# Scores of 64 contraction rows in row halves of TensorE, weights times values alternating between heads, and decay levels without their masked blocks

## The chip, the cores and the metric

The kernel runs on one core of one Trainium2 chip. The metric is the device time of one launch in microseconds, taken as the median of several runs. TensorE does the matrix products, VectorE (DVE in the profile), ScalarE (ACT) and GpSimd (POOL) the elementwise work, and SyncE (SP) issues the DMAs.

## The reference

The input is one sequence of 256 tokens of width 1024. Two transformer layers come first, each with modulation vectors from `silu(c) @ w_mod`, layer norms and a SwiGLU feed-forward; then one hybrid layer with 16 meta tokens in front, and a final norm. All of it is float32. Four places matter here.

- Layer 0, stick-breaking attention (8 heads of 64): `z = q k^T / 8` for the past keys, and the weights are `exp(log_sigmoid(z) + suffix sum of log_sigmoid(-z))`, then weights times values.
- Layer 0, DSA attention (8 heads of 64 with one shared key and value): an index score, `sum over 4 index heads of relu(q_idx k_idx^T) * w`, selects 64 keys for each query, and a softmax over those follows.
- Layer 1, differential attention (8 heads, two components of 64 each): `softmax(q0 k0^T) - lam * softmax(q1 k1^T)`, causal, times values of width 128.
- The hybrid layer's gated recurrence (8 heads of 128): `S_t = diag(f_t) S_{t-1} + k_t v_t^T`, `o_t = S_t^T q_t`.

```
s = einsum('bqhcd,bshcd->bhcqs', q, k) * d ** -0.5
p = softmax(where(causal, s, -inf))
a = p[:, :, 0] - lam * p[:, :, 1]
```

## The kernel before

Activations are kept transposed: channels on the 128 partitions, tokens in the free dimension. A weight slab (128 x 2048) is loaded by DMA into `stage`, split into a high part `whi` (ScalarE) and a rest `wlo` (VectorE), and each projection does three products per block of 128 channels (`mm3`, `group`, `gemm_pair`); the first seven slabs are loaded whole and multiplied in plain f32. The attention products are plain f32 too, which TensorE runs as two records each.

The order of the work isn't the order of the source. Every operation goes to `Plan.record`, which notes its engine, an estimate of its cost, its dependences and its place; `Plan.order` then simulates the engines, and on each takes the ready operation with the lowest place (with a small part for the length of what hangs on it); `issue` emits them in that order at line 433, so nearly all rows of the profile bear that line. Attention is written as generators (`gen_topk`, `gen_dsa`, `gen_sb`, `gen_diff`, `gen_hgrn`); `spin(3)` between the projections takes three steps of the oldest generator, and `BIAS` shifts the places of its operations (75 for the top-k, DSA and decay generators, 0 for stick-breaking and differential scores). The planner counts writes to one PSUM bank as dependent on each other; all eight banks are one pool, `pa`. SBUF tiles come from pools too: `w4` (19 of 1096 columns), `w2` (5 of 512), `w1`, `sm`.

The places that the change touches:

- Scores of two heads (or components) of 64 rows are one product over all 128 rows. The moving operand is a zero-padded block tile: `kz_d`, `kz_i` (lines 954 to 966), `qz` (1082 to 1093) and `kz` (1284 to 1298) hold one head's 64 rows in one half of the columns and the other's in the other half, with zeros between (GpSimd memsets). `gen_topk` (992), `gen_dsa` (1055), `gen_sb` (1128, 1129) and `gen_diff` (1249) use them. A mask is added to the scores in PSUM by a bf16 product with the identity.
- Products of weights and values for two heads write the two halves of the output partitions of one bank (1071 to 1075, 1150 to 1155), head by head.
- `gen_diff` handles one head in four steps (two query tiles, each with scores and softmax, then transposes).
- `gen_hgrn` builds the decayed attention matrix in levels of block size B = 1 to 64 within tiles of 128 tokens (1524 to 1552): for each level `Xt` holds decayed keys in the even blocks and decayed queries in the odd ones, eight products `Xt^T Xt` (128 x 128) go into two banks, and two masked copies (`copy_predicated` with `msk`) take the blocks that belong to the level.

Of the kernel before, what the change touches and what calls it, by code (L numbers as in the profile page):

```python
# [14 lines left out]
ALU = mybir.AluOpType  # L15
# [44 lines left out]
BUFS = {'w4': 19, 'w2': 5, 'w1': 11, 'sm': 16, 'stage': 3, 'mst': 3, 'whi': 6, 'wlo': 6}  # L60
# [45 lines left out]
class Plan:  # L106
# [74 lines left out]
    def cost(self, eng, op, writes, reads):  # L181
# [255 lines left out]
def kernel(ctx, tc, io, out):  # L437
# [516 lines left out]
    kz_t = w4("kzt")  # L954
    kz_d = kz_t[:, 0:512]
    kz_i = kz_t[:, 512:1024]
    G.memset(kz_t[:, 0:1024], 0.0)
# [6 lines left out]
    for a, kz, r0 in ((0, kz_d, 0), (1, kz_i, 64)):  # L964
        for b in range(2):
            V.tensor_add(kz[b * 64:b * 64 + 64, b * S:(b + 1) * S], t1[r0:r0 + 64, 0, :], t2[r0:r0 + 64, 0, :])
# [18 lines left out]
    def gen_topk():  # L985
        for t in range(2):
            nk = 128 * (t + 1)
            s = bias[:, t, :]
            for c in range(2):
                ps = bank("ps_i")  # L990
                o = two(ps[:, :2 * nk])
                T.matmul(o, qi[:, c * S + t * 128:c * S + t * 128 + 128], two(kz_i)[:, :, :nk], start=True, stop=True)
                r = two(w2("rl")[:, :2 * nk])
                A.activation(r, o, AF.Relu)
                for a in range(2):
                    if c == 0 and a == 0:
                        V.tensor_scalar(s[:, :nk], r[:, 0, :], wix[:, t, 0:1], 0.0, op0=ALU.mult, op1=ALU.add)
                    else:
                        V.scalar_tensor_tensor(s[:, :nk], r[:, a, :], wix[:, t, 2 * c + a:2 * c + a + 1], s[:, :nk],
# [48 lines left out]
    def gen_dsa():  # L1048
        for t in range(2):
            nk = 128 * (t + 1)  # L1050
            PT = [w4c(f"pt{t}{i}", S) for i in range(t + 1)]
            for j in range(4):
                ps = bank("ps_i")
                o = two(ps[:, :2 * nk])
                T.matmul(o, qd[j // 2][:, (j % 2) * S + t * 128:(j % 2) * S + t * 128 + 128], two(kz_d)[:, :, :nk],
                         start=True, stop=False)
                T.matmul(o, identb, biasb[:, t, None, :nk].to_broadcast([128, 2, nk]), start=False, stop=True)
                e = two(w2("e"))
                ls = softmax_pair(e, o, nk)
                for a in range(2):  # L1060
                    if a < EACT:
                        A.activation(e[:, a, :nk], e[:, a, :nk], AF.Copy, scale=ls[:, a:a + 1])
                    else:
                        V.tensor_scalar(e[:, a, :nk], e[:, a, :nk], ls[:, a:a + 1], None, op0=ALU.mult)
                for st in range(t + 1):
                    pt = bank("ps_t")
                    for a in range(2):
                        T.transpose(pt[:, a * 128:a * 128 + 128], e[:, a, st * 128:st * 128 + 128], ident)
                    A.activation(PT[st].rearrange("p j (a q) -> p a j q", a=2)[:, :, j, :], two(pt[:, :256]), AF.Copy)
                yield  # L1070
            ps = bank("ps_o")
            for a in range(2):
                for st in range(t + 1):
# [50 lines left out]
    def gen_sb():  # L1124
        for j in range(4):
            qzj = two(qz[j // 2][:, (j % 2) * 512:(j % 2) * 512 + 512])
            za, zb = bank("ps_z"), bank("ps_z")
            T.matmul(two(za), ks[:, j, 0:128], qzj, start=True, stop=False, skip_group_check=True)
            T.matmul(two(zb[:, :256]), ks[:, j, 128:256], qzj[:, :, 128:256], start=True, stop=False, skip_group_check=True)
            for ap in (two(za)[:, :, 0:128], two(zb[:, :256])):  # L1130
                T.matmul(ap, identb, strib[:, None, :].to_broadcast([128, 2, 128]), start=False, stop=True,
                         skip_group_check=True)
            sp = w4("sp")
            A.activation(sp[:, 0:512], za, AF.Abs)
            A.activation(sp[:, 512:768], zb[:, :256], AF.Abs)
            A.activation(sp[:, :768], sp[:, :768], AF.Exp, scale=-1.0)
            A.activation(sp[:, :768], sp[:, :768], AF.Ln, bias=1.0)
            V.scalar_tensor_tensor(sp[:, 0:512], za, 0.0, sp[:, 0:512], op0=ALU.max, op1=ALU.add)
            V.scalar_tensor_tensor(sp[:, 512:768], zb[:, :256], 0.0, sp[:, 512:768], op0=ALU.max, op1=ALU.add)
            yield  # L1140

            T.matmul(za, C("tn"), sp[:, 0:512], start=False, stop=False, skip_group_check=True)
# [728 lines left out]
```

## Time and profile before

| | |
|---|---|
| median of 3 runs | 1158.2 us (1157.85 to 1158.86) |
| profiled execution, its own time | 1161.2 us |
| its span, first to last instruction | 1159.4 us |
| mean granted TensorE clock | 0.99 |
| TensorE busy | 1127.6 us, 97% |
| weight loads busy | 1079.3 us, 93% |
| VectorE busy | 912.1 us, 79% |
| ScalarE busy | 723.1 us, 62% |

PE is the matrix product itself, PEld the loading of its stationary operand. A matmul's record lasts beyond its place in the pipeline, so the pace is read from start to start and not from the record's length. A chain of waits is followed back from the last instruction to what released each step. Tiles are named by their pool: `pa` is any PSUM bank, `w` any working tile, `cst` the constants.

### The profile page before, as it was taken

How to read it: one execution, taken by the hardware profiler on the slowest of the kernel's cores; microseconds unless marked ns; L12 is line 12 of the kernel's file. 1: busy time of each engine (PE TensorE's matmuls, PEld its weight loads, DVE VectorE, ACT ScalarE, POOL GpSimd, SP SyncE). 2: the span in 40 equal slices, each digit the busy share in tenths (PEclk: the TensorE clock that was granted, in tenths of full speed). 3: DMA queues.
4: the chain of work that ended last, by engine and by line, in shares of the span. 5: the costliest groups of instructions: out<-in, count | busy, mean ns of one | idle time of the engine just before them, and what ended most of it. 6: DMA issues, size and time to landing. Idle time of an engine off the chain costs nothing.

```text
span 1159.4 us, 21967 instructions
## 1 busy us (share of the span) xinstructions
PE 1127.6 (97%) x8787; PEld 1079.3 (93%) x8787; DVE 912.1 (79%) x1764; ACT 723.1 (62%) x1314; POOL 12.4 (1%) x18
## 2 busy tenths in 40 slices
PE   5999999999999899999999999999999999999997
PEld 4886799999998779999999999999999999999996
DVE  6799899888989899995557696996579886767652
ACT  3558677444459987764445377876757765555541
POOL 1010000000010000000000000000000000000000
PEclk9999999999999999999999999999999998999998
DMA  9938748998983244585554524344433434555441
GB/s 349 411 125 316 258 146 326 331 338 308 338 327 121 87 168 146 200 309 183 178 200 168 198 82 173 120 165 156 180 110 124 168 110 146 207 187 184 169 164 37
DMA packets 42247, 232.27 MB, mean 200 GB/s; under 512 B 4641, under 2 KB 6177, under 8 KB 24097
## 3 DMA queue, kind: packets, MB, share of 16 engines
q1 hardware_dynamic: 42144, 230.87, 54.9%
q8 instruction: 69, 1.13, 0.4%
q14 instruction: 34, 0.27, 0.1%
HBM read 229.81 MB, written 1.05 MB: 199 GB/s over the span
## 4 chain that ended last, share of the span: by engine, by line
PE 82%; DVE 9%; ACT 5%; DMA 3%; issue 1%; SPq 0%; DVEq 0%; ACTq 0%
PE pa L433 82%; DVE w L433 5%; ACT w L433 4%; DMA mst<-in_wmod_dram 2%; DVE wlo L433 2%; DVE mst L433 1%; ACT whi L433 1%; DVE sm L433 1%; DMA w<-in_pos_dram 1%; DMA w<-in_xT_dram 1%; DVE stage L433 0%; SPq L433 0%; ACT sm L433 0%; DVE mw L433 0%; DVEq L1867 0%
## 5 line engine op out<-in xcount | busy, mean ns | idle before, releaser
L433 PE MATMUL pa<-w,whi 128*128 128x256 f32 (+4 forms) x5104 | 920.3, 288 | 9.3 <-DMA whi<-in_w_dram 7.4
L433 PEld LDWEIGHTS pa<-w,whi 128*128 128x128 f32 x5104 | 771.2, 190 | 18.5 <-ACT w L433 6.7
L433 PE MATMUL pa<-w,wlo 128*128 128x256 f32 (+3 forms) x2608 | 665.7, 290 | 2.2 <-DVE wlo L433 2.2
L433 ACT ACTIVATE whi<-stage 128x1024 fp32r<-128x1024 f32 (+1 forms) x330 | 338.7, 1041 | 254.8 <-PE pa L433 226.6
L433 PEld LDWEIGHTS pa<-w,wlo 128*128 128x128 f32 x2608 | 467.2, 190 | 9.0 <-DVE wlo L433 4.0
L433 DVE TENSOR_TENSOR wlo<-stage,whi 128x1024 fp32r<-128x1024 f32 (+1 forms) x330 | 392.8, 1201 | 93.1 <-ACT whi L433 90.8
L433 ACT ACTIVATE w<-w 128x256 fp32r<-128x256 f32 (+9 forms) x257 | 117.1, 468 | 71.6 <-DVE w L433 68.0
L433 DVE TENSOR_TENSOR w<-w,w 128x256 fp32r<-128x256 f32 (+6 forms) x323 | 144.8, 465 | 10.9 <-ACT w L433 9.0
L433 ACT ACTIVATE w<-pa 128x256 f32<-128x256 f32 (+12 forms) x298 | 108.0, 390 | 47.1 <-PE pa L433 41.4
L433 DVE SCALAR_TENSOR_TENSOR mst<-mst,scb 128x1024 f32<-128x1024 f32 x90 | 108.7, 1221 | 9.2 <-DMA mst<-in_wmod_dram 8.9
L433 DVE TENSOR_TENSOR w<-w,pa 128x256 f32<-128x256 f32 (+2 forms) x146 | 58.7, 418 | 56.7 <-PE pa L433 52.0
L432 ACT ACT_TABLE_LOAD x61 | 78.3, 1283 | 1.8 <-PEq L1861 0.7
L433 PE MATMUL pa<-w,w 128*128 128x128 f32 (+8 forms) x340 | 68.6, 334 | 3.0 <-issue 1.6
L433 PEld LDWEIGHTS pa<-w,w 128*128 128x128 f32 (+4 forms) x340 | 41.9, 174 | 13.1 <-issue 7.1
L433 PE MATMUL pa<-cst,w 128*128 128x1 f32 (+4 forms) x236 | 38.8, 255 | 3.3 <-ACT w L433 3.3
L433 PEld LDWEIGHTS pa<-cst,w 128*128 128x128 f32 (+2 forms) x236 | 29.0, 158 | 10.0 <-ACT w L433 6.1
L433 PE MATMUL pa<-w 128*128 128x128 f32 x240 | 34.6, 275 | 0.0
L433 PE MATMUL pa<-whi,w 128*128 128x512 f32 x96 | 32.6, 423 | 0.0
L433 PEld LDWEIGHTS pa<-w 128*128 128x128 f32 x240 | 31.3, 191 | 0.0
L433 DVE SCALAR_TENSOR_TENSOR w<-pa,vec,w 128x256 f32<-128x256 f32 (+1 forms) x48 | 23.1, 483 | 6.6 <-PE pa L433 5.7
L433 DVE SCALAR_TENSOR_TENSOR w<-pa,mod,w 128x256 f32<-128x256 f32 x32 | 15.0, 481 | 14.8 <-PE pa L433 14.8
L433 DVE COPY_PREDICATED w<-msk,pa 128x512 f32<-128x512 uint8 x28 | 20.5, 737 | 3.9 <-PE pa L433 3.8
(144 smaller groups left out, 478.1 us busy)
## 6 DMA issues: line engine op xcount, KB each, us to landing
mst<-in_wmod_dram SPq DMA_DIRECT2D x90, 512.0 KB, 5.5
stage<-in_wgu_dram SPq DMA_DIRECT2D x44, 1024.0 KB, 5.0
stage<-in_wi_dram SPq DMA_DIRECT2D x36, 1024.0 KB, 4.8
stage<-in_wup_dram SPq DMA_DIRECT2D x22, 1024.0 KB, 4.8
stage<-in_wd_dram SPq DMA_DIRECT2D x24, 896.0 KB, 4.5
stage<-in_w_dram SPq DMA_DIRECT2D x15, 1024.0 KB, 6.7
stage<-in_wo_dram SPq DMA_DIRECT2D x12, 1024.0 KB, 4.8
stage<-in_wd_dram SPq DMA_DIRECT2D x12, 1024.0 KB, 5.4
```

Of the source, the lines that this page charges most:

```text
L432: self.nc.scalar.preload_act_table_set(tables[i])
L433: fn(*[real(a) for a in args], **{k: real(a) for k, a in kw.items()})
```

## The change

Scores: `scores` makes two products of 64 rows per pair of heads, one on partitions 0 to 63 and one on 64 to 127, into two banks (one per head); two pairs share the two banks. The zero-padded tiles and their memsets go. `gen_diff` takes two heads in one generator of six steps; DSA takes two pairs together. Products of weights and values are written alternately for the two heads. A decay level multiplies the first 128 - B columns of `Xt` with its odd blocks alone, eight products of 64 columns into one bank, with one masked copy. The planner halves its estimate for f32 products of 64 rows, and pool `w2` has six buffers.

```diff
-BUFS = {'w4': 19, 'w2': 5, ...
+BUFS = {'w4': 19, 'w2': 6, ...
...
-                return max(214.0, 4 * n / 2.4 + 5)
+                return max(214.0, 4 * n / 2.4 + 5) / (2 if reads[0].shape[0] == 64 else 1)
...
+    def scores(o, c, left, right, stop=False):
+        for a in range(2):
+            r = slice(a * 64, a * 64 + 64)
+            T.matmul(o[a][:, c, :], left[r], right[r], start=c == 0, stop=stop, skip_group_check=True)
...
-    kz_t = w4("kzt")
-    kz_d = kz_t[:, 0:512]
-    kz_i = kz_t[:, 512:1024]
-    G.memset(kz_t[:, 0:1024], 0.0)
+    kz_d, kz_i = w2("kd2")[:, :S], w2("ki2")[:, :S]
...
+            o = [two(bank("ps_i")[:, :2 * nk]) for _ in range(2)]
             for c in range(2):
-                ps = bank("ps_i")
-                o = two(ps[:, :2 * nk])
-                T.matmul(o, qi[:, c * S + t * 128:c * S + t * 128 + 128], two(kz_i)[:, :, :nk], start=True, stop=True)
+                scores(o, c, qi[:, c * S + t * 128:c * S + t * 128 + 128], kz_i[:, :nk], c == 1)
...
-            for j in range(4):
-                ps = bank("ps_i")
-                o = two(ps[:, :2 * nk])
-                T.matmul(o, qd[j // 2][:, (j % 2) * S + t * 128:(j % 2) * S + t * 128 + 128], two(kz_d)[:, :, :nk],
-                         start=True, stop=False)
-                T.matmul(o, identb, biasb[:, t, None, :nk].to_broadcast([128, 2, nk]), start=False, stop=True)
-                e = two(w2("e"))
-                ls = softmax_pair(e, o, nk)
...
+            for i in range(2):
+                o = [two(bank("ps_i")[:, :2 * nk]) for _ in range(2)]
+                for c in range(2):
+                    scores(o, c, qd[i][:, c * S + t * 128:c * S + t * 128 + 128], kz_d[:, :nk])
+                es = []
                 for a in range(2):
...
+                    T.matmul(o[a], identb, biasb[:, t, None, :nk].to_broadcast([128, 2, nk]), start=False, stop=True,
+                             skip_group_check=True)
+                    e = two(w2("e"))
+                    ls = softmax_pair(e, o[a], nk)
...
-            for a in range(2):
-                for st in range(t + 1):
+            for st in range(t + 1):
+                for a in range(2):
                     T.matmul(ps[a * 64:a * 64 + 64, :].rearrange("p (j q) -> p j q", j=4), vtok[:, st, 0:64],
...
-    qz = [w4("qz0"), w4("qz1")]
-    ks = w4c("ksb", S)
-    for i in range(2):
-        G.memset(qz[i], 0.0)
+    qs, ks = w4c("qsb", S), w4c("ksb", S)
...
-            ps = two(next_pair())
-            for c in range(2):
-                for a in range(2):
-                    A.activation(qz[i][a * 64:a * 64 + 64, c * 512 + a * S:c * 512 + a * S + S], ps[a * 64:a * 64 + 64, c, :],
-                                 AF.Copy, scale=0.125)
+            ps = next_pair()
+            A.activation(qs[:, 2 * i:2 * i + 2, :], two(ps), AF.Copy, scale=0.125)
...
-            T.matmul(two(za), ks[:, j, 0:128], qzj, start=True, stop=False, skip_group_check=True)
-            T.matmul(two(zb[:, :256]), ks[:, j, 128:256], qzj[:, :, 128:256], start=True, stop=False, skip_group_check=True)
...
+            z = [bank("ps_z") for _ in range(2)]
+            for a in range(2):
+                r = slice(a * 64, a * 64 + 64)
+                T.matmul(z[a][:, 0:256], ks[r, j, 0:128], qs[r, j, :], start=True, stop=False, skip_group_check=True)
+            for a in range(2):
+                r = slice(a * 64, a * 64 + 64)
+                T.matmul(z[a][:, 256:384], ks[r, j, 128:256], qs[r, j, 128:256], start=False, stop=False, skip_group_check=True)
...
             for a in range(2):
                 h = 2 * j + a
-                T.matmul(ps[a * 64:a * 64 + 64, 0:256], vsb[:, 0, h * 64:h * 64 + 64], w[:, a * 256:a * 256 + 256],
+                T.matmul(ps[a * 64:a * 64 + 64, 0:256], vsb[:, 0, h * 64:h * 64 + 64], w[:, a * 384:a * 384 + 256],
                          start=True, stop=False, skip_group_check=True)
+            for a in range(2):
+                h = 2 * j + a
                 T.matmul(ps[a * 64:a * 64 + 64, 128:256], vsb[:, 1, h * 64:h * 64 + 64],
-                         w[:, 512 + a * 128:512 + a * 128 + 128], start=False, stop=True, skip_group_check=True)
+                         w[:, a * 384 + 256:a * 384 + 384], start=False, stop=True, skip_group_check=True)
...
-    def gen_diff(h, q, kz):
+    def gen_diff(h, qk):
...
+            o = [two(bank("ps_i")[:, :2 * nk]) for _ in range(2)]
+            for c in range(2):
+                scores(o, c, qk[c][:, 0, t * 128:t * 128 + 128], qk[c][:, 1, :nk])
+            es = []
+            for a in range(2):
+                T.matmul(o[a][:, :, t * 128:nk], identb, causb[:, None, :].to_broadcast([128, 2, 128]), start=False,
+                         stop=True, skip_group_check=True)
+                e = two(w2("e"))
+                es.append((e, softmax_pair(e, o[a], nk)))
+            (e0, l0), (e1, l1) = es
+            for c in range(2):
+                V.tensor_scalar(e1[:, c, :nk], e1[:, c, :nk], l1[:, c:c + 1], nlam, op0=ALU.mult, op1=ALU.mult)
+                V.scalar_tensor_tensor(e0[:, c, :nk], e0[:, c, :nk], l0[:, c:c + 1], e1[:, c, :nk], op0=ALU.mult, op1=ALU.add)
             yield
...
-            G.memset(kzt[:, 0:1024], 0.0)
...
-        V.tensor_add(q, parts[0][0], parts[0][1])
-        for a in range(2):
-            V.tensor_add(kz[a * 64:a * 64 + 64, a * S:a * S + S], parts[1][0][a * 64:a * 64 + 64],
-                         parts[1][1][a * 64:a * 64 + 64])
-        bg.append((gen_diff(h, q, kz), BIAS["diff"]))
+        if h % 2 == 0:
+            qk0 = qk
+        else:
+            bg.append((gen_diff(h - 1, (qk0, qk)), BIAS["diff"]))
...
-                for hp in range(2):
-                    ps = bank("ps_h")
-                    for a in range(2):
-                        for t in range(2):
-                            xs = Xt[:, 2 * hp + a, t * 128:t * 128 + 128]
-                            T.matmul(ps[:, (a * 2 + t) * 128:(a * 2 + t) * 128 + 128], xs, xs, start=True, stop=True,
-                                     skip_group_check=True)
-                    V.copy_predicated(quads(At, hp), msk[:, None, lv * 128:lv * 128 + 128].to_broadcast([128, 4, 128]),
-                                      ps.rearrange("p (a b) -> p a b", b=128))
-                    yield
+                n = 128 - B
+                ps = bank("ps_h")[0:n, :].rearrange("p (q i b) -> p q i b", q=8, b=B)
+                for h in range(4):
+                    for t in range(2):
+                        xs = Xt[:, h, t * 128:t * 128 + 128]
+                        T.matmul(ps[:, 2 * h + t], xs[:, 0:n], xs.rearrange("p (i c b) -> p c i b", c=2, b=B)[:, 1],
+                                 start=True, stop=True, skip_group_check=True)
+                V.copy_predicated(tiles(At)[0:n].rearrange("p q (i c b) -> p q c i b", c=2, b=B)[:, :, 1],
+                                  msk[0:n, None, lv * 128:lv * 128 + 128].to_broadcast([n, 8, 128]).rearrange(
+                                      "p q (i c b) -> p q c i b", c=2, b=B)[:, :, 1], ps)
+                yield
```

## Rows read from the trace of the kernel before

**Rows 1.** The page: busy time of each engine with its share of the span and its instructions, and the shares of the chain that ended last.
```profile
PE 1127.6 (97%) x8787; PEld 1079.3 (93%) x8787; DVE 912.1 (79%) x1764; ACT 723.1 (62%) x1314; POOL 12.4 (1%) x18
...
PE 82%; DVE 9%; ACT 5%; DMA 3%; issue 1%; SPq 0%; DVEq 0%; ACTq 0%
```

**Rows 2.** The chain of waits in the window from 60 to 150 us, layer 0's attention and the products behind it: shares, then pieces with start (us), length (us) and what ran.
```profile
by line: DMA mst<-in_wmod_dram 21.4%; PE pa L433 20.4%; DVE mst L433 16.9%; DVE w L433 12.3%; DVE sm L433 9.4%; DVE wlo L433 9.2%; ACT whi L433 4.4%; ACT w L433 2.9%; issue 2.7%; DVE mw L433 0.5%; DVE biasb L433 0.2%; DVEq L433 0.0%; ACTq L
...
116.75 6.43 DMA mst<-in_wmod_dram
...
124.83 13.74 PE pa L433 x94
```

**Rows 3.** The same in the window from 340 to 440 us, layer 1's attention.
```profile
by line: PE pa L433 51.4%; ACT w L433 26.1%; DVE w L433 9.1%; ACT whi L433 6.8%; issue 3.3%; DVE wlo L433 2.4%; DVE sm L433 0.8%; ACT sm L433 0.3%
...
403.25 36.81 PE pa L433 x203
```

**Rows 4.** The same in the window from 690 to 960 us, the hybrid layer's projections with the decay levels among them.
```profile
by line: PE pa L433 97.6%; DVE wlo L433 1.3%; ACT w L433 0.4%; issue 0.3%; DVE w L433 0.2%; DVE sm L433 0.2%; ACT sm L433 0.1%; DVEq L433 0.0%
```

**Rows 5.** Busy time by stretch: the window, its length, busy us (and instructions) of PE, PEld, DVE, ACT and POOL, the granted clock, the DMA share and GB/s.
```profile
380.00:390.00 10.00, 8.40 (x52) 6.30 (x52) 8.09 (x20) 9.70 (x24) 0.00 (x0) 1.00 0.30 105
...
700.00:720.00 20.00, 19.86 (x162) 19.27 (x161) 14.51 (x32) 15.70 (x23) 0.00 (x0) 0.91 0.59 211
720.00:760.00 40.00, 40.00 (x341) 40.00 (x341) 36.33 (x56) 31.41 (x39) 0.00 (x0) 1.00 0.30 107
```

**Rows 6.** TensorE's instructions in order of time in layer 1's attention: start (us), length (us), engine, line, operation, tiles, shape, count. `pa<-w,w` with 512 or 256 columns is a score product (two records), `causb` the mask that follows it. The first two score products behind 403.25 us and the last are shown; there are six, three of each width.
```profile
407.92 0.59 PE L433 MATMUL pa<-w,w 128*128 128x256 f32 x2
408.35 0.27 PE L433 MATMUL pa<-causb,identb 128*128 128x256 bf16 x1
...
411.47 1.02 PE L433 MATMUL pa<-w,w 128*128 128x512 f32 x2
412.33 0.27 PE L433 MATMUL pa<-causb,identb 128*128 128x256 bf16 x1
...
423.57 1.02 PE L433 MATMUL pa<-w,w 128*128 128x512 f32 x2
```

**Rows 7.** The same around one head pair's products of weights and values (128*64: 64 of the 128 output columns of the array); four of the eight records have 256 columns and four have 128, the merged row names the first.
```profile
128.42 0.28 PE L433 MATMUL pa<-w,wlo 128*128 128x256 f32 x1
128.54 0.27 PE L433 MATMUL pa<-w,whi 128*128 128x256 f32 x1
128.75 0.88 PE L433 MATMUL pa<-w,w 128*64 128x256 f32 x8
129.55 0.62 PE L433 MATMUL pa<-w,whi 128*128 128x256 f32 x3
130.01 0.28 PE L433 MATMUL pa<-w,wlo 128*128 128x256 f32 x1
```

**Rows 8.** The same around one small product of 32 rows and 32 output columns in the decay part.
```profile
777.23 0.40 PE L433 MATMUL pa<-w,w 32*32 32x128 f32 x2
777.56 0.51 PE L433 MATMUL pa<-w,wlo 128*128 128x258 f32 x2
777.91 0.52 PE L433 MATMUL pa<-w,whi 128*128 128x258 f32 x3
```

**Rows 9.** The same for one decay level of the second half (`pa<-w`, sixteen records) with the next row, for sums with one data column and 128 weight columns (a few of the thirty have 32), and weight loads of 32 columns (PEld).
```profile
712.59 0.52 PEld L433 LDWEIGHTS pa<-w,w 128*32 128x32 f32 x14 [0.21 <-issue]
...
871.01 1.95 PE L433 MATMUL pa<-w 128*128 128x128 f32 x16
872.71 0.48 PE L433 MATMUL pa<-w,whi 128*128 128x258 f32 x2
...
953.33 3.41 PE L433 MATMUL pa<-cst,w 128*128 128x1 f32 x30
```

**Rows 10.** The same for the level of block size 64 in the first half: the first and the last of the six runs in which its sixteen records come, and the projections' product behind the first.
```profile
770.72 0.38 PE L433 MATMUL pa<-w 128*128 128x128 f32 x2
770.86 0.37 PE L433 MATMUL pa<-w,whi 128*128 128x260 f32 x1
...
773.14 0.61 PE L433 MATMUL pa<-w 128*128 128x128 f32 x4
```

**Rows 11.** Groups of instructions with shapes kept apart: line, engine, operation, tiles, shape, count, then busy us and mean ns of one, idle time before them and what ended it.
```profile
L433 DVE TENSOR_TENSOR w<-w,w 128x256 f32<-128x256 f32 x99 | 40.9, 422 | 3.3 <-ACT w L433 2.4
...
L433 DVE TENSOR_TENSOR w<-w,w 128x512 f32<-128x512 f32 x49 | 32.6, 687 | 2.7 <-ACT w L433 2.7
...
L433 DVE COPY_PREDICATED w<-msk,pa 128x512 f32<-128x512 uint8 x28 | 20.5, 737 | 3.9 <-PE pa L433 3.8
...
L433 ACT ACTIVATE w<-pa 128x512 f32<-128x512 f32 x22 | 12.7, 597 | 11.3 <-PE pa L433 11.3
...
L433 ACT ACTIVATE w<-pa,sm 128x256 f32<-128x256 f32 x24 | 11.2, 473 | 1.9 <-DVE sm L433 1.8
...
L433 ACT ACTIVATION_READ_ACCUMULATOR w<-pa,sm 128x1 f32 x48 | 9.7, 203 | 0.0
...
L433 ACT ACTIVATE w<-pa,sm 128x128 f32<-128x128 f32 x24 | 8.6, 365 | 3.9 <-DVE sm L433 3.9
...
L433 DVE TENSOR_TENSOR w<-w,w 64x256 f32<-64x256 f32 x20 | 8.3, 417 | 0.3
...
L433 ACT ACTIVATE w<-pa 64x256 f32<-64x256 f32 x8 | 3.0, 378 | 2.5 <-PE pa L433 2.5
```

More of the change, by code (lines that the diff above doesn't have):

```diff
@@ L59 @@
 AHEAD = 1
-BUFS = {'w4': 19, 'w2': 5, 'w1': 11, 'sm': 16, 'stage': 3, 'mst': 3, 'whi': 6, 'wlo': 6}
+BUFS = {'w4': 19, 'w2': 6, 'w1': 11, 'sm': 16, 'stage': 3, 'mst': 3, 'whi': 6, 'wlo': 6}
 NST = 6
@@ L1071, in gen_dsa @@
             ps = bank("ps_o")
-            for a in range(2):
-                for st in range(t + 1):
+            for st in range(t + 1):
+                for a in range(2):
                     T.matmul(ps[a * 64:a * 64 + 64, :].rearrange("p (j q) -> p j q", j=4), vtok[:, st, 0:64],
@@ L1133, in gen_sb @@
[L1133 to L1139, printed above, removed]
+            z = [bank("ps_z") for _ in range(2)]
@@ new lines, in gen_sb @@
+            for a in range(2):
[4 more added lines that the diff above has]
+                T.matmul(z[a][:, 256:384], ks[r, j, 128:256], qs[r, j, 128:256], start=False, stop=False, skip_group_check=True)
+            sp = two(w4("sp")[:, :768])
+            for a in range(2):
+                T.matmul(z[a][:, 0:512].rearrange("p (b n) -> p b n", b=2)[:, :, 0:128], identb,
+                         strib[:, None, :].to_broadcast([128, 2, 128]), start=False, stop=True, skip_group_check=True)
+                A.activation(sp[:, a, :], z[a][:, :384], AF.Abs)
@@ L1140, in gen_sb @@
+            A.activation(sp, sp, AF.Exp, scale=-1.0)
+            A.activation(sp, sp, AF.Ln, bias=1.0)
+            for a in range(2):
+                V.scalar_tensor_tensor(sp[:, a, :], z[a][:, :384], 0.0, sp[:, a, :], op0=ALU.max, op1=ALU.add)
             yield
-            T.matmul(za, C("tn"), sp[:, 0:512], start=False, stop=False, skip_group_check=True)
-            T.matmul(two(za)[:, :, 128:256], C("neg1"), two(sp[:, 512:768]), start=False, stop=True, skip_group_check=True)
-            T.matmul(zb[:, :256], C("tn"), sp[:, 512:768], start=False, stop=True, skip_group_check=True)
@@ L1145, in gen_sb @@
             w = w4("wsb")
-            A.activation(w[:, 0:512], za, AF.Exp)
-            A.activation(w[:, 512:768], zb[:, :256], AF.Exp)
+            for a in range(2):
+                T.matmul(z[a][:, :384], C("tn"), sp[:, a, :], start=False, stop=False, skip_group_check=True)
+                T.matmul(z[a][:, 128:256], C("neg1"), sp[:, a, 256:384], start=False, stop=True, skip_group_check=True)
+                A.activation(w[:, a * 384:a * 384 + 384], z[a][:, :384], AF.Exp)
             yield
@@ L1280 @@
             ps = gemm_pair(X)
-        q = w1("qh")[:, :S]
         if h % 2 == 0:
-            aTt, kzt = w4("aT"), w4("kz")
-            G.memset(kzt[:, 0:1024], 0.0)
+            aTt, kzt = w4("aT"), w4("qk")
         aT[h] = aTt[:, (h % 2) * 384:(h % 2) * 384 + 384]
-        kz = kzt[:, (h % 2) * 512:(h % 2) * 512 + 512]
+        qk = two(kzt[:, (h % 2) * 512:(h % 2) * 512 + 512])
         if ps is not None:
             t1, t2 = rope_parts(two(ps), 2)
-            parts = [(t1[:, c, :], t2[:, c, :]) for c in range(2)]
+            V.tensor_add(qk, t1, t2)
         else:
-            parts = []
             for c in range(2):
                 t1, t2 = rope_parts(pss[2 * (h - 2) + c][:, None, :], 1)
-                parts.append((t1[:, 0, :], t2[:, 0, :]))
-        V.tensor_add(q, parts[0][0], parts[0][1])
-        for a in range(2):
-            V.tensor_add(kz[a * 64:a * 64 + 64, a * S:a * S + S], parts[1][0][a * 64:a * 64 + 64],
-                         parts[1][1][a * 64:a * 64 + 64])
-        bg.append((gen_diff(h, q, kz), BIAS["diff"]))
+                V.tensor_add(qk[:, c, :], t1[:, 0, :], t2[:, 0, :])
+        if h % 2 == 0:
+            qk0 = qk
+        else:
+            bg.append((gen_diff(h - 1, (qk0, qk)), BIAS["diff"]))
         if h >= 2:
@@ L1510, in gen_hgrn, with tiles @@
         V.memset(Sx, 0.0)
+        def tiles(t):
+            return t.rearrange("p a b -> p (a b)").rearrange("p (q n) -> p q n", n=128)
         def quads(t, hp):
@@ L1542, in gen_hgrn @@
             if lv < 7:
[L1543 to L1552 removed]
+                n = 128 - B
[8 more added lines that the diff above has]
+                                      "p q (i c b) -> p q c i b", c=2, b=B)[:, :, 1], ps)
+                yield
             else:
```

55 lines of the change are left out of this document (21 added, 34 removed).

## The prediction

> **What bounds the kernel now.** I read the page first: TensorE is busy for 97% of the span and its weight loads for 93%, and the chain that ended last lies on PE for 82% of it [rows 1]. The reader should see there that most of the span is priced in TensorE time, and that 18% is not. The next view is the chain of waits, stretch by stretch, around the places that the change touches. In layer 0's attention (60 to 125 us) the chain has 20.4% on PE in a window of 90 us, and these 18.4 us are the two stretches from 124.83 us on: before that it runs over VectorE (the top-k steps, the `wlo` splits, the products into `mst`) and over DMAs of the modulation weights that land 6.4 us after what they waited for [rows 2]. In layer 1's attention the chain is largely on ScalarE and VectorE from 348 to 403 us (26.1 and 9.1% of a window of 100 us, with 6.8% for the `whi` copies), and on PE for 36.81 us from 403.25 us on [rows 3]. In the decay part of the second block it is PE for 97.6% [rows 4]. The stretches agree: in 720 to 760 us PE and its weight loads are busy for all 40 us with VectorE at 36.33, and in 380 to 390 us PE has 8.40 of 10 and ScalarE 9.70 [rows 5]. So a product that becomes shorter is worth its time after 403 us and in the decay levels, and in the two other stretches next to nothing: there something else ends last.
>
> **Scores of 64 rows.** A score product over the whole array with 512 output columns takes 0.86 us of TensorE (from 411.47 to the next instruction at 412.33), with 256 columns 0.43 (407.92 to 408.35) [rows 6]; the cost follows the columns, and half of the rows multiply zeros. The change has two products of half the columns in the two row halves. No f32 product in the trace uses a half of the rows, so I bound it. The nearest rows are the products of weights and values, which use 64 of the 128 output columns: eight records, whose times one after another would be 4 x 0.213 + 4 x 0.107 = 1.28 us (half of the 0.43 above for a record of 256, a quarter for 128), stand between 128.75 and 129.55 us, thus in 0.80 us [rows 7]. The two halves ran at once: 0.64 us each and 0.16 besides. If row halves do likewise, a score costs half; if they don't, it costs what it costs now. I take half and keep both ends.
>
> The same rows show what going into such a part of the array and back costs. Before the block TensorE started its next record after 0.21 us where 0.12 is usual (128.54 to 128.75); the 0.16 follows, and behind it three records take 0.46 (129.55 to 130.01) where three of 0.12 would be 0.36. That is 0.09 + 0.16 + 0.10 = 0.35 us for one trip. A single small product of 32 rows pays nearly as much: 0.33 from 777.23 to 777.56 for two records of 0.11, then 0.35 for two at 0.12, so 0.22 and what its entry cost [rows 8]. I take 0.35 per uninterrupted run of tiled products; 0.2 and 0.45 are the bounds.
>
> The Trainium skill says in TensorEngine Tiling (Array Packing), section Tiling Modes, that changing the tiling mode (not just the tile) drains TensorE and that different tiles then work in parallel. Rows 7 and 8 agree with both halves of it; it speaks against short tiled products among full ones, which is the second rival below.
>
> Now the sum, part by part. Index scores: four products before (2 x 0.43 + 2 x 0.86 = 2.58 us), two groups after, at best 1.29 + 2 x 0.35. DSA: 5.16 before, 2.58 + 4 x 0.35 after. Stick-breaking: per head pair a product of 512 and one of 256 columns, 1.29; after 0.64 + 0.35; four times. These are 12.9 us before and 9.95 after, 3.0 less, and all of it lies before 125 us, where the chain is on VectorE and DMAs: I count 0, with -3.0 as the end if PE decides there after all. Differential scores: 8 x (0.43 + 0.86) = 10.3 us before, 5.2 + 8 x 0.35 = 8.0 after. Of these, three of each width start after 403.25 us (the first at 407.92, the last at 423.57 [rows 6]): 3.9 us before, half of it and four runs after, 1.95 + 4 x 0.35 = 3.35: **-0.5**. The rest lies under the ScalarE chain and counts 0.
>
> **Products of weights and values.** The source has head 0's two products ahead of head 1's, and the planner keeps writes to one bank in that order; yet rows 7 show them in 0.80 us, the halves side by side. There is nothing left to gain from alternating them: 0, at most the 0.16 in each of six such blocks, 1 us, most of it where PE is off the chain. The Trainium skill has in TensorE: Matmul & The Clock Gate, section Part 3: Packing small matmuls — row/col tiling, that matmuls start and end in program order; by that the old order would have kept the halves apart, and alternating would save 1.28 - 0.64 = 0.64 us a block of stick-breaking. The measured 0.80 decides.
>
> **Decay levels.** Per half, seven levels of eight products, two records each. Sixteen records in a row take 1.70 us (871.01 to 872.71), 0.106 each [rows 9]. Would half the columns make them faster? A product with one column and 128 weight columns still takes 0.11 (30 in 3.41 us), while loads of 32 weight columns follow each other at 0.037 (14 in 0.52 us) [rows 9]. So the weight columns set the pace, not the 64 data columns. The change cuts them to 128 - B: by a straight line between the two, a record falls by (0.106 - 0.037)/96 = 0.0007 us per column, in the six levels with B = 1 to 32 by 63 columns together: 0.045 x 16 records x 2 halves = **-1.45 us**. At B = 64 the weights are 64 columns wide and the product becomes a tiled one: 16 x 0.06 = 0.97 us against 1.70, less 0.35 for each run. In the second half such levels run in one piece (rows 9), -0.38; in the first half the level of that block size is in six runs, split by products of the projections (the first at 770.72, the last at 773.14) [rows 10]: 6 x 0.35 - 0.73 = +1.37 if it stays so, -0.38 if it becomes one. I take the middle, three runs, +0.3. Together **-1.5**, between -2.2 and -0.5. Data columns in strides of two are not in the trace; up to twice the time per data column they would stay under the weight load.
>
> **VectorE, ScalarE, GpSimd.** The masked copies fall from 28 x 737 ns to 14 of the same 512 elements [rows 11], 10.3 us less on VectorE; even at twice the time for strided rows they cost no more than now. PE covers all of it (rows 4), so 0, unless a `wlo` split was late: VectorE's share of that chain is 1.3 + 0.2%, 4 us at most. Rope's three additions (one of 128 x 256 at 422 ns, two of 64 x 256 at 417, 1.26 us) become one of 687 ns; the copies of the stick-breaking queries fall from 8 x 378 to 2 x 597 ns on ScalarE; GpSimd's memsets go [rows 11]. They shorten the chain of the 348 to 403 us stretch by some 0.5 us for the heads up to there. Against it, two heads are now taken in one step, and three steps per `spin` bring a generator of six steps per pair faster ahead than one of four per head: at the same place about one head's softmax more is queued on ScalarE, ahead of the next head's rope. A head's exponentials are 2 x (473 + 365) + 4 x 203 = 2.5 us [rows 11]. ScalarE has them to do anyway; what they delay is between 0 and 2.5. With the 0.5 to 1 us saved I take 0.
>
> **Sum.** -0.5 - 1.5 = -2.0 us. The profiled execution took 1161.2 us with a span of 1159.4, so it would take 1159.2; the median of the runs is 1158.2, so I predict **1156.2**. Less than 0.2% (2.3 us) is no change that a measurement of this kernel can tell.
>
> **Rivals.** (A) TensorE's time counts everywhere: also the 3.0 us before 125 and the other 1.8 us of the differential scores (10.3 - 8.0 less the 0.5). Then -6.8: 1151.4. For it speaks PE's 97%, against it rows 2 and 3. (B) The tiled products don't stay together: slower. The planner orders PE by the place in the program (shifted for the background by its bias) and knows no price for a trip; rows 10 show products of one level each between projections. If all 16 differential score products after 403 us and all 16 of the last tiled level make a trip each, nothing overlaps and 32 x 0.35 = 11.2 stand against 1.45 + 2 x 0.73 = 2.9: +8.3, 1166.5. It decides from about 14 trips on, where 0.35 each eats 1.95 + 2.9 = 4.9. Against it: products of one group have neighbouring places and the differential scores have no bias. (C) Row halves don't run at once, so the change doesn't do what it says: the differential scores cost +1.4 instead of -0.5, in sum -0.1: 1158.1. (D) ScalarE's extra head ahead is not hidden: -2.0 + 2.5, 1158.7, with two heads 1161.2. Besides, the planner's order is made anew for the whole program, and the granted clock falls to its lower level (1.2 GHz) here and there: the mean of 0.91 over 700 to 720 us [rows 5] is 20 x 0.09 = 1.8 us, which can come or go.
>
> **Chances.** Forecast 0.47 (its own range 1153.5 to 1159.5), A 0.18, B 0.12, C 0.10, D 0.13. Half of the forecast's weight lies below 1155.9, which with A makes 0.42 for faster; B, a third of D and the upper edge of the others make 0.24 for slower; 0.34 stays within 0.2%. The range 1150 to 1163 leaves out most of B and the far ends of A and D.
>
> **What would show it.** After: a stick-breaking or DSA score group in about half its time plus a gap of some 0.1 us at each end (else C); runs of 64-row products in pieces of four (else B); the decay records at 0.1 us with 124 weight columns and 0.06 with 64; PE's chain as long as before in 348 to 403 us, and PE with more idle time before 125 us. The prediction is wrong if the span shrinks by more than 6 us, or if the stretch between 348 and 440 us alone changes by more than 3.

## The result and the profile after

The changed kernel takes 1167.49 us (median; 1166.22 to 1168.68), the kernel before 1158.03 beside it: a ratio of 1.0088 with a 95% interval of 1.0075 to 1.0102. It is slower by 0.9%, where 1156.2 was predicted and 1150 to 1163 given as the range. The profiled execution after took 1167.49 us with a span of 1165.7; that of the kernel before, with 1161.2 us, was 3 us longer than its median, so the two traces show 6.3 of the 9.5 us.

The page of the changed kernel, the lines that answer to [rows 1]: TensorE is busy 10 us longer, and the chain that ended last is on it for 89% where it was 82.

```profile
PE 1137.4 (98%) x8867; PEld 1082.1 (93%) x8867; DVE 901.0 (77%) x1736; ACT 722.0 (62%) x1308; POOL 4.9 (0%) x11
...
PE 89%; DVE 5%; ACT 3%; DMA 1%; issue 0%; SPq 0%; DVEq 0%; ACTq 0%
```

The chain of the changed kernel from 60 to 150 us, which answers to [rows 2]. VectorE and DMAs ended last there before; now it is one piece of TensorE of 46 us, and PE has 75.1% of the window where it had 20.4.

```profile
by line: PE pa L433 75.1%; ACT w L433 7.5%; DMA mst<-in_wmod_dram 7.5%; DVE mst L433 6.5%; DVE w L433 1.4%; DVE wlo L433 1.3%; issue 0.5%; DVE sm L433 0.4%; DVE mw L433 0.0%; DVEq L433 0.0%
...
59.98 46.17 PE pa L433 x227
...
118.82 6.73 DMA mst<-in_wmod_dram
...
128.68 21.38 PE pa L433 x150
```

Busy time by stretch in layer 0's attention, first of the kernel before, then of the changed one (columns as in [rows 5]). Before, TensorE was idle for 1.83 and 2.30 us of the first and the last stretch; after, the first is full.

```profile
70.00:90.00 20.00, 18.17 (x108) 15.40 (x107) 19.79 (x58) 8.55 (x28) 1.44 (x2) 1.00 0.46 161
90.00:110.00 20.00, 20.00 (x86) 12.74 (x85) 18.73 (x39) 17.83 (x46) 0.00 (x0) 1.00 0.90 337
110.00:130.00 20.00, 17.70 (x109) 12.23 (x109) 16.87 (x34) 14.05 (x27) 0.00 (x0) 1.00 0.82 289
```

```profile
70.00:90.00 20.00, 20.00 (x112) 16.75 (x111) 16.33 (x50) 6.89 (x18) 1.44 (x2) 1.00 0.42 147
90.00:110.00 20.00, 20.00 (x99) 12.43 (x98) 16.86 (x34) 16.19 (x48) 0.00 (x0) 1.00 0.72 243
110.00:130.00 20.00, 18.04 (x107) 12.15 (x107) 17.20 (x34) 13.36 (x29) 0.00 (x0) 1.00 0.86 318
```

What fills it is seen in TensorE's instructions of the changed kernel (columns as in [rows 6]). The four products of 64 rows of a score group mostly don't stand side by side: of the forty in layer 0, 18 come alone between other work, like the two here between products of the projections, and four groups of ten stay whole.

```profile
77.62 0.28 PE L433 MATMUL pa<-w,wlo 128*128 128x256 f32 x1
77.74 0.28 PE L433 MATMUL pa<-w,whi 128*128 128x256 f32 x1
77.94 0.48 PE L433 MATMUL pa<-w,w 64*128 64x128 f32 x2
78.36 0.38 PE L433 MATMUL pa<-w,whi 128*128 128x256 f32 x1
78.67 0.49 PE L433 MATMUL pa<-w,w 64*128 64x128 f32 x2
```

From 77.94 to 78.67 is one such product and one projection's record: 0.73 us, less 0.12 for the record 0.61, which is what a lone product costs. It is half of a product that took 0.43 as a whole [rows 6]. In layer 0, 76 of the 80 score records stand in 24 uninterrupted runs between other work; with the records beside them that start late on their account they take 19.7 us of TensorE, where all of layer 0's scores took 12.9 before. In layer 1 it is 15 runs.

The two traces have the same 7856 records of the projections, so each can be laid beside its twin (times below are those of the kernel before). After layer 0 (at 152 us) the changed kernel is 4.2 us late and at 357 us 5.0; behind layer 1 (455 us) 8.9; from 703 to 945 us, in the decay levels, it falls from 8.5 to 6.8. Layer 1 has a stretch at the lower level of the clock (1.2 GHz) that it hadn't before, 6.8 us from 381.2 us on (0.66 over ten us, where [rows 5] have 1.00), which is worth at most half of that:

```profile
380.00:390.00 10.00, 8.59 (x44) 6.89 (x44) 9.14 (x22) 9.22 (x24) 0.00 (x0) 0.66 0.50 186
```

### The profile page after: what moved, and what is told of

It is laid out like the page before. It is cut to its first block, busy times and chain, and to the rows that moved or that the text cites. A ratio compares the mean times of both kernels' runs of the same rounds, so it can differ in the third digit from the quotient of the medians.

```text
span 1165.7 us, 22104 instructions
## 1 busy us (share of the span) xinstructions
PE 1137.4 (98%) x8867; PEld 1082.1 (93%) x8867; DVE 901.0 (77%) x1736; ACT 722.0 (62%) x1308; POOL 4.9 (0%) x11
## 4 chain that ended last, share of the span: by engine, by line
PE 89%; DVE 5%; ACT 3%; DMA 1%; issue 0%; SPq 0%; DVEq 0%; ACTq 0%
PE pa L433 89%; DVE w L433 3%; ACT w L433 3%; DVE wlo L433 1%; DMA whi<-in_w_dram 1%; DMA mst<-in_wmod_dram 1%; DVE mst L433 1%; DVE sm L433 0%; ACT whi L433 0%; SPq L433 0%; DVE stage L433 0%; ACT sm L433 0%; DVEq L1875 0%; DVE cosT L433 0%; DVE lam L433 0%
## 5 line engine op out<-in xcount | busy, mean ns | idle before, releaser
L433 ACT ACTIVATE w<-w 128x256 fp32r<-128x256 f32 (+8 forms) x257 | 117.3, 468 | 71.3 <-DVE w L433 65.8
L433 DVE TENSOR_TENSOR w<-w,w 128x256 fp32r<-128x256 f32 (+7 forms) x309 | 141.1, 472 | 10.9 <-ACT w L433 9.1
L433 ACT ACTIVATE w<-pa 128x256 f32<-128x256 f32 (+11 forms) x292 | 107.3, 391 | 52.0 <-PE pa L433 46.6
L433 PE MATMUL pa<-w,w 128*128 128x128 f32 (+8 forms) x348 | 57.4, 307 | 0.7 <-DVE w L433 0.3
L433 PEld LDWEIGHTS pa<-w,w 128*128 128x128 f32 (+5 forms) x348 | 39.6, 172 | 12.3 <-issue 4.6
L433 PE MATMUL pa<-w 64*128 64x256 f32 (+9 forms) x304 | 41.3, 288 | 2.4 <-DVE w L433 1.9
L433 PEld LDWEIGHTS pa<-w 64*128 64x128 f32 (+8 forms) x304 | 33.5, 182 | 7.8 <-issue 4.2
L433 DVE SCALAR_TENSOR_TENSOR w<-w,vec,w 128x258 f32<-128x258 f32 (+2 forms) x44 | 20.8, 481 | 1.9 <-ACT w L433 1.4
```

The source lines that it names most:

```text
L433: fn(*[real(a) for a in args], **{k: real(a) for k, a in kw.items()})
```

## The experiments

Each kernel was timed against the kernel before on the same chip. Executions of one kernel lay up to 10 us apart (1153.6 to 1163.4 for the kernel before in the third set), and the intervals are 2.5 to 4.6 us wide.

**The decay levels alone** (`e1_decay_only`): the last hunk of the change, put into the kernel before.

> The kernel before with only the decay levels changed; scores and products of weights and values as before. From the alignment of the two traces the decay part alone gives 1.7 to 1.9 us back, so 1156.2 us with either theory of the loss. If the gain in the decay part was only the clock drop that no longer fell there, the time stays at 1158.

Measured: 1158.66 us against 1157.37, ratio 1.0005 (0.9990 to 1.0020). No gain: the 1.7 us of the traces' comparison weren't the levels'.

**The groups in one step** (`e2_glued`): a step of the planner may now hold several products, which are issued with nothing between them.

```diff
+    def together(self, done):
...
+        calls, self.joint = self.joint, None
+
+        def fn(*args):
+            for i, (f, _, kw) in enumerate(calls):
+                f(*args[3 * i:3 * i + 3], **kw)
...
+            run.together(0)
             for c in range(2):
                 scores(o, c, qk[c][:, 0, t * 128:t * 128 + 128], qk[c][:, 1, :nk])
+            run.together(1)
```

> The changed kernel, with the four score products of a group (and the sixteen records of the decay level of 64) issued as one step of the planner, so that nothing falls between them. Theory of the trips (each lone tiled product among full ones pays 0.4 to 0.6 us, and that made PE the bound in both attention parts): nearly all of the 8.9 us lost there goes, 1155 to 1158 us. Rival, the clock that fell in layer 1's attention or the softmax of two heads moved ahead on ScalarE: at least the 3.9 us of layer 1 stay, 1162 us or more. Rival, the row halves' price itself (also in one piece): 1164 or more.

Measured: 1153.82 us, ratio 0.9964 (0.9950 to 0.9978), and some 14 us less than the change. A DSA group of this kernel, the counterpart of the products above, with the row before and the one behind it:

```profile
81.84 0.28 PE L458 MATMUL pa<-w,wlo 128*128 128x256 f32 x1
82.05 0.71 PE L275 MATMUL pa<-w,w 64*128 64x128 f32 x8
82.70 0.39 PE L458 MATMUL pa<-biasb,identb 128*128 128x256 bf16 x2
```

Four products in 0.65 us and one late start (0.21 for 0.12), where four lone ones cost 4 x 0.61. Layer 0's score groups now stand in 9 runs of 9.4 us (72 records; the last group follows products of weights and values at once). In the chain from 60 to 150 us the engines share the window again:

```profile
by line: PE pa L458 51.3%; ACT w L458 11.9%; DVE w L458 8.7%; DMA mst<-in_wmod_dram 7.6%; DVE sm L458 6.4%; DVE mst L458 5.3%; DVE wlo L458 4.0%; ACT whi L458 2.2%; issue 1.5%; PE pa L275 1.2%; DVE biasb L458 0.2%; ACTq L458 0.0%
```

**Layer 0 as before, layer 1 as before** (`e3_no_L0`, `e4_no_L1`): the hunks of one layer taken out of the change.

> The changed kernel with layer 0's attention as before (index, DSA and stick-breaking scores, and the order of its products of weights and values); layer 1 and the decay levels changed. If the losses add up as in the alignment, 1167.5 - 5.0 = 1162.5 us. If layer 0's loss is made good later on anyway, it stays at 1167.

> The changed kernel with layer 1's differential scores as before; layer 0 and the decay levels changed. If the losses add up, 1167.5 - 3.9 = 1163.6 us, and the clock's fall at 381 us is gone. If it stays at 1167, layer 1's loss was not its own.

Measured: 1164.05 us (ratio 1.0059, 1.0043 to 1.0075) and 1166.47 (1.0068, 1.0048 to 1.0087). Neither part alone is free, and the two don't add up: by the ratios 6.8 and 7.9 us more than before, with 10.2 for the whole change.

**Which groups** (`e5_glue_scores`, `e6_full64`, `e7_glue_L0`): the scores in one step but not the decay level of 64; the same with that level's weights kept 128 columns wide; and layer 0's groups alone in one step.

```diff
-                n = 128 - B
+                n = 128 - B if B < 64 else 128
```

> As the version whose score groups and whose decay level of 64 are each one step (1153.8 us), but with the sixteen records of that level loose again, as in the change. Theory of the trips: in the changed kernel the level of the first half stands in seven runs and takes 4.07 us more than the projections around it, in one run 1.27; so 2.8 us come back, 1156.6 us. If trips cost only where they meet the attention's own chain, it stays at 1153.8.

> Score groups as one step; the decay level of 64 loose, but with 128 weight columns, so that it is no tiled product (its upper rows are computed and left out by the mask's zeros). Theory of the trips: such a lone product pays no trip, a level costs about 1.75 us instead of 4.07 and 1.27, so against the loose tiled level -2.3 + 0.5: 1154.7 us, about one us above the version with the level in one piece. If the tiled level's width mattered and not its trips, 1157 or more.

> The changed kernel with only layer 0's score groups (index, DSA, stick-breaking) each one step; layer 1's scores and the decay level loose as in the change. Theory of the trips: layer 0's share of the loss goes and layer 1's stays, 1167.5 - 5 = 1162.5 us, between the version with all groups in one step and the change. If one layer's pieces are all that matters, it is either 1157 (layer 0) or 1167 (layer 1).

Measured: 1158.16 (ratio 1.0003, 0.9986 to 1.0020), 1155.80 (0.9977, 0.9966 to 0.9988) and 1158.96 (1.0003, 0.9988 to 1.0018). The order of the first two is as expected, but both lie further above `e2_glued`: 4.3 us where 2.8 were expected, and 2.0 where it was 0.9. Their levels explain 2.2 and 1.2 of that (table below); the clock differs too, and in `e5_glue_scores` the runs at a mean granted clock of 0.993 took 1153.9 us, those at 0.987 took 1160.4 to 1162.4. Layer 0's groups in one step take 8.5 us off the change. `e5_glue_scores` is that kernel with layer 1's products in one step as well, and by the medians it is 0.8 us faster, within the noise.

**Layer 0 or layer 1 loose, all else in one step** (`e10_loose_L0`, `e11_loose_L1`).

> As the version at 1153.8 us (score groups and the level of 64 in one step each), but layer 0's score groups loose. In the trace of the change these stand in 24 runs and take 21.6 us, in one step each 9 runs and 9.5. Theory of the trips on the chain of layer 0: nearly all of the change's loss is here, 1162 to 1164 us. If the layers share it, 1157 to 1159.

> As the version at 1153.8 us, but layer 1's score groups loose: 18.3 us of TensorE instead of 10.1. ScalarE's chain covers most of it in 348 to 403 us: 1153.8 to 1156 us. If layer 1 costs what the alignment of the two traces first said (3.9 us), 1157.7.

Measured: 1163.37 (ratio 1.0057, 1.0037 to 1.0077) and 1155.40 (0.9984, 0.9971 to 0.9996). Layer 0's lone products cost 9.5 us against `e2_glued`, layer 1's 1.6, with intervals that overlap. The traces give layer 1 more. `e2_glued`, `e5_glue_scores` and `e6_full64` show the same sequence of TensorE records up to 711 us, and `e7_glue_L0` and `e11_loose_L1` the same as each other, with layer 1 loose. From 357 to 455 us, laid beside the kernel before, the first three gain 0.02, 1.45 and 0.25 us, though the clock fell there twice, once and once; the other two lose 2.04 and 2.05 without a fall. So the loose products cost 2.1 to 3.5 us there; by 703 us the three had one more fall each, and the other two none, and the gain is mostly gone. The chain from 60 to 150 us of `e10_loose_L0` has the piece of 46 us of the changed kernel again:

```profile
by line: PE pa L458 92.2%; ACT w L458 7.9%; issue 0.1%
...
59.85 46.15 PE pa L458 x227
106.00 0.02 issue
106.03 7.13 ACT w L458 x19
```

In `e2_glued` PE has 51.3% of that window (above). Laid beside it, `e10_loose_L0` is 4.9 us late at 357 us; 2 us more come in layer 1, whose code is the same.

**The decay levels with the level of 64 in one step** (`e9_dec_glued`), in the kernel before.

> The kernel before with only the decay levels changed, and the level of 64 as one step. In the traces so far the fourteen levels take 25.0 us before, 26.0 with the level of 64 loose, 23.2 with it in one piece. TensorE sets the end in that part, so -1.8 us: 1155.8 us; if the reordering around it eats the gain, 1157.7 as before.

Measured: 1156.36 us against 1157.01, ratio 0.9986 (0.9972 to 1.0001): by the ratio 1.6 us, about the size expected (1.8), by the medians 0.65, and not clear of no change. The traces are clearer. TensorE sets the end in this part, so what a kernel gains between the same two projection records (703.2 and 944.7 us of the kernel before) is compared with two things: the time of its fourteen levels (from the record ahead of a level to the second behind it, less 0.12 for each projection record in it), and the number of times that the clock fell to its lower level in that stretch, each time for 3.4 us, so for 1.7 us of work.

| kernel | levels, us | falls | difference to before, us | from levels and falls |
|---|---|---|---|---|
| before | 25.00 | 2 | | |
| the change | 25.00 | 1 | -1.74 | -1.7 |
| e1_decay_only | 24.98 | 2 | -0.02 | 0.0 |
| e2_glued | 22.95 | 0 | -5.27 | -5.5 |
| e5_glue_scores | 25.11 | 0 | -3.13 | -3.3 |
| e6_full64 | 24.11 | 1 | -2.60 | -2.6 |
| e9_dec_glued | 23.01 | 1 | -3.58 | -3.7 |

The two account for all seven within 0.2 us. As the change has them the levels gain nothing; with the level of 64 in one step they gain 2.0 us, and with that level untiled 0.9. One fall that the change lacks is seen in the stretch from 710 to 720 us, of the kernel before and of the changed one (the clock is the third number from the end):

```profile
710.00:720.00 10.00, 9.86 (x79) 9.28 (x78) 8.41 (x16) 6.96 (x9) 0.00 (x0) 0.83 0.64 235
```

```profile
710.00:720.00 10.00, 10.00 (x87) 10.00 (x86) 6.72 (x20) 7.58 (x12) 0.00 (x0) 1.00 0.35 125
```

**Weights and values** (`e8_glue_pv`, `e12_pv_order`): each head pair's block in one step as well, alternating as in the change, and head by head as before. With nothing to hold them together the change, and `e2_glued` too, had split two of the stick-breaking blocks, so that the first product stood alone (in `e2_glued` 0.58 + 0.79 us for 0.80).

> Score groups and the decay level of 64 in one step as in the version at 1153.8 us, and the products of weights and values of one head pair in one step too. There two stick-breaking blocks stand in two pieces, 0.58 + 0.79 us and a second way in and out where one piece takes 0.80; theory of the trips: 0.8 us each, so 1152.2 us. If VectorE and the DMAs set the end there, it stays at 1153.8, or gets slower, since the step waits for the last of its operands.

> As the version with the products of weights and values in one step too (1152.65 us), but head by head as before, not alternating. The two halves ran side by side in either order in the traces (0.808 us a block head by head, 0.801 alternating), so no difference: 1152.7 us. If program order keeps the halves apart, each of the four stick-breaking blocks takes 0.5 us longer and the two of DSA more: 1155 us or more.

Measured: 1152.65 (ratio 0.9952, 0.9935 to 0.9969), the fastest version, and 1154.50 (0.9973, 0.9960 to 0.9986); the intervals overlap. Outside these blocks both issue their products in the same order, so the traces can tell. One block, alternating and then head by head, with the next row:

```profile
125.05 0.87 PE L275 MATMUL pa<-w,w 128*64 128x256 f32 x8
125.85 0.39 PE L458 MATMUL pa<-w,whi 128*128 128x256 f32 x1
```

```profile
125.72 0.88 PE L275 MATMUL pa<-w,w 128*64 128x256 f32 x8
126.53 0.39 PE L458 MATMUL pa<-w,whi 128*128 128x256 f32 x1
```

0.80 and 0.81 us. Of the 3.1 us between the two profiled executions 0.7 are there by 133 us (0.4 from the start of the program on), 1.5 come at 398 and some 1.2 at 661 us, where the clock fell in the second kernel and not in the first. In the stretches around them, first of the alternating kernel, then of the other:

```profile
395.00:405.00 10.00, 8.84 (x66) 8.00 (x66) 8.72 (x17) 9.85 (x25) 0.00 (x0) 1.00 0.29 106
652.00:662.00 10.00, 10.00 (x85) 9.98 (x84) 6.44 (x26) 2.48 (x7) 0.00 (x0) 1.00 0.55 205
```

```profile
395.00:405.00 10.00, 8.85 (x56) 7.91 (x55) 8.23 (x18) 8.60 (x20) 0.00 (x0) 0.83 0.23 84
655.00:665.00 10.00, 10.00 (x72) 10.00 (x71) 5.53 (x24) 1.56 (x6) 0.00 (x0) 0.83 0.45 175
```

**Layer 0 as before with layer 1 in one step, and the planner's old price** (`e13_oldL0_glueL1`, `e14_old_price`), for what the others left open.

```diff
-                return max(214.0, 4 * n / 2.4 + 5) / (2 if reads[0].shape[0] == 64 else 1)
+                return max(214.0, 4 * n / 2.4 + 5)
```

> Layer 0's attention as before, layer 1's score groups each one step, the decay level of 64 loose; it differs from the run at 1164.1 us (layer 0 as before, layer 1 loose) in layer 1 alone. Theory that there too the lone products are the loss: 1158 to 1159 us, as with the decay levels alone. Rival, that a new order of layer 0, whose code is that of before, is the loss (its profile lay 3.2 us behind already at 134 us): it stays at 1162 or more.

> The changed kernel, but the planner prices a product of 64 rows as before, at its full time of 214 ns or more, not at half of it. Theory of the trips: a price does not keep a group together, so about as many lone products and 1164 to 1168 us. Rival, the planner is misled by the halved price: 1160 or less.

Measured: 1161.31 (ratio 1.0040, 1.0024 to 1.0056) and 1166.39 (1.0069, 1.0049 to 1.0089). The price isn't it: layer 0's scores stand in 26 runs between other work, where the change has 24, and the time is that of the change. The first lies between its two theories. With layer 1's products in one step some 2 of the 6.8 us that `e3_no_L0` lost are gone. Part of the other 4.6 came with layer 0's old code, which the planner issued in another order from 88 us on, once something behind it had changed: it was 3.4 and 2.2 us late by 134 us in the two profiles, where the two kernels with only the decay levels changed, in the old order, were 1.1 and 0.8 us early. The rest isn't placed.

## Why the prediction was wrong

**The step that failed** is "all of it lies before 125 us, where the chain is on VectorE and DMAs: I count 0". Its bound was -3.0, worked out for groups that stay together. They came apart, and the part that was said to be covered grew by some 7 us (12.9 to 19.7), over a cover of at most 4.1 us of idle TensorE (1.83 + 2.30 in the windows above, of which 1.96 are idle after, too). TensorE became the bound there: the changed kernel left layer 0 about 5 us late in the trace, and keeping layer 0's groups in one step, alone, takes 8.5 us off the median. A cost counted at nothing needed its cover priced from above as well.

**Rival B was the right one, put in the wrong place.** It was given 0.12, priced for products after 403 us and in the last decay level; that its 1166.5 us lies near the measured 1167.5 is luck, as the loss came mainly from other trips, in layer 0. Against it stood that "products of one group have neighbouring places and the differential scores have no bias". Neighbouring places didn't keep a group together. By the planner's code each step goes to the ready operation with the earliest place, and other work can have a place among a group's; this was read from the code, and of it only the price was tested (`e14_old_price`). The rows that showed the result were there: one level in six runs [rows 10]. The price of a trip was right. A lone product of two records pays 0.61 - 2 x 0.107 = 0.40 us on top of its own time, near the 0.35; the level of 64, in seven runs, takes 3.29 us, and its sixteen records at 0.058 (the median where they stand in one piece) leave 0.34 a run. The Trainium skill says in TensorEngine Tiling (Array Packing), section Tiling Modes, that a change of the tiling mode drains TensorE; these numbers agree, and they give its price here.

**Differential scores, -0.5.** In one step they take 8.2 us in `e13_oldL0_glueL1` (8.0 was worked out), loose 15.1 in `e11_loose_L1`. What that costs is 1.6 us by the medians and 2.1 to 3.5 by the traces, of 7 us of TensorE: the rest is covered, as the prediction said for the stretch up to 403 us. The stretch changed by more than the 3 us that the prediction named as a sign of being wrong: 3.8 us from 357 to 455 us in the comparison of the two traces. Without a fall of the clock `e7_glue_L0` and `e11_loose_L1`, whose products are loose too, lose 2.0 there; that leaves some 1.8 for the fall of 6.8 us at 381, as far as different orders can be compared.

**Decay levels, -1.5: measured 0.0.** Two terms were off. The six levels of B = 1 to 32 gave 1.0 us (21.4 to 20.4), not 1.45. The direction was right: the weight columns set the pace. In the changed kernel's second half a level with 124 columns takes 1.66 us where one with 128 took 1.70 [rows 9], and the level of 64, in one piece, 1.07:

```profile
882.46 1.84 PE L433 MATMUL pa<-w 128*124 128x64 f32 x16
884.12 0.36 PE L433 MATMUL pa<-w,whi 128*128 128x258 f32 x1
...
909.24 1.15 PE L433 MATMUL pa<-w 128*64 128x64 f32 x16
910.31 0.39 PE L433 MATMUL pa<-w,whi 128*128 128x258 f32 x1
```

And the level of 64 cost 1.0 us more in the two halves together (3.29 + 1.27 for 2 x 1.78), not 0.1 less: "I take the middle, three runs" met seven in the first half. Here is how they begin:

```profile
763.15 0.45 PE L433 MATMUL pa<-w 128*64 128x64 f32 x4
763.52 0.38 PE L433 MATMUL pa<-w,whi 128*128 128x258 f32 x1
763.84 0.33 PE L433 MATMUL pa<-w 128*64 128x64 f32 x2
764.09 0.39 PE L433 MATMUL pa<-w,wlo 128*128 128x258 f32 x1
```

**What held.** VectorE's masked copies fell from 20.5 us to 12.6 and not by the 10.3 worked out, as two of the strided forms take 1.33 us apiece; in TensorE's time it shows nowhere. Row halves run at once (0.65 us for four products whose times one after another are 0.85), so rival C is out. The order of weights and values is worth 0.007 us a block. The prediction set against it the rule that matmuls start and end in program order (the Trainium skill, TensorE: Matmul & The Clock Gate, section Part 3: Packing small matmuls — row/col tiling); the loss that it worked out from that rule for the order head by head doesn't appear, in blocks of 0.81 us. Rival D doesn't appear: with all groups in one step and the heads taken in pairs the kernel is 0.2 us behind the one before at 455 us, with falls of the clock at 107, 366 and 400 us among it. Rival A is out too: where the groups were whole, shorter scores in layer 0 gained nothing clear (at 152 us `e2_glued` is 0.2 us late, with a fall of 6.8 us on the way, and `e7_glue_L0` without one 0.4 early; kernels with the same sequence of records up to there lie up to 1.3 us apart), not the 3.0 that A counted.

**What stays open.** Only some 5 of the 8.5 to 9.5 us that layer 0's lone products cost are seen in layer 0's own stretch. In `e10_loose_L0` 2 more come in layer 1, in code that is the same, with an order that the planner makes anew for the whole program; no run holds that order fixed. Part of the rest can be the clock's. Its mean over the runs was 0.9895 for the change (4 runs) and 0.9923 for `e7_glue_L0` (12), 0.9894 for `e10_loose_L0` (7) and 0.9918 for `e2_glued` (6); by an estimate from these, 0.0028 and 0.0024 of a span, at most 3.3 and 2.8 us. Whether lone products make the clock fall more often, no run shows.

## What to carry to other kernels

A smaller product in a part of the array is worth its arithmetic only in one piece with others of its kind: alone between full products it cost 0.61 us here where the full-width product it halves took 0.43. Before such a change, look in the trace of before at whether the scheduler leaves groups whole, and if not, make the group one step; that alone turned +9.5 us into -3.5 (ratio 0.9964), and with the products of weights and values into -5.0 (0.9952). And before a difference of two profiled executions is given to a step, count where the clock fell in each, and set the mean clocks of the runs beside a difference of medians.

## What was not expected of the hardware

Besides a last time at its end, the granted clock falls to its lower level for 3.4 or 6.8 us at a time, one to five times in a profiled execution: five times in `e2_glued`, once in `e7_glue_L0`, twice and five times in two kernels that differ only inside six blocks. The places recur, but not in every execution: the two attention parts (107 to 128 and 364 to 400 us), then 661 to 671, 713 to 724, 846 to 857 and 948 to 967 us. In the ten us before a fall TensorE was busy for 60 to 92% in the attention parts, and for 97 to 100% in the others. Each 3.4 us cost 1.2 to 1.7 where TensorE set the end. That is as large as the effects this change was made of, and it made the decay levels of the change look 1.7 us better than they are. What made it fall in one execution and not in another, no run here shows.
